# Two plain column tiles instead of four in the first up projection, and a beginning of both up projections ordered by planned times

## The chip, the cores and the metric

The kernel runs on one core of one Trainium2 chip. The metric is the device time of one execution in microseconds; lower is better. The kernel before was timed in three runs, and one more execution was taken with the hardware profiler.

## The reference, cut to what matters

One layer of a hybrid decoder on 512 rows of 1024 columns, all in float32:

```python
def swiglu(x, w_gate, w_up, w_down):
    return (jax.nn.silu(x @ w_gate) * (x @ w_up)) @ w_down

for l in range(DEPTH):                                    # DEPTH = 1
    x = x + 0.5 * swiglu(rmsnorm(x, ffn1_norm[l]), ffn1_wg[l], ffn1_wu[l], ffn1_wd[l])
    x = x + hybrid_mixer(rmsnorm(x, mix_norm[l]), ...)
    x = x + 0.5 * swiglu(rmsnorm(x, ffn2_norm[l]), ffn2_wg[l], ffn2_wu[l], ffn2_wd[l])
return rmsnorm(x, final_norm)
```

The gate and the up matrix of each SwiGLU are 1024 x 2816, so 22 column tiles of 128 each. The change lies in the products with these matrices, in the first SwiGLU and in the second.

## The kernel before, in words

**Precision.** TensorE multiplies float32 in three passes: each operand is split into a rounded part and a remainder (`wh` and `wl` for weights, `yh` and `yl` for the normalised input), and the product of the two remainders is left out. The rounding is a ScalarE copy (`ACTIVATE`), the remainder a VectorE subtraction that waits for it (`wsplit`, L237).

**Plain tiles.** A plain product multiplies one column tile of the gate or of the up matrix (1024 x 128) with all 512 rows: 8 steps of 128 inputs, three matmuls of 512 columns each, 24 in all (`gemm`, L254). The input here is x times the gain; the division by the root mean square is put off: VectorE multiplies the sums with `rstd`. `rstd` comes from `norm_steps` (L289): eight matmuls with a constant matrix (`mean`), a ScalarE square root, a VectorE reciprocal, four transposes on TensorE and a ScalarE copy.

**Units.** The other column tiles are done by a scheme of the Strassen and Winograd kind. A unit takes two column tiles of one matrix (unit `w` those of the gate if `w` is even, those of the up matrix if odd) and cuts inputs, rows and columns in halves. Seven products of half the inputs, half the rows and one tile's columns then stand for eight. Each product has a weight operand (a block of the weights or a sum of blocks: a11, a12, s1 to s4, a22) and a moving operand (`n11`, `b21`, `t2`, `t1`, `r`, `q`, `n22`, each of four parts j). The moving operands are the same for all units, and are built once at the beginning of a projection, out of x, gain and `rstd`, by `moving_operands` (L341): VectorE forms two scaled operands `ca` and `cb` for each j and their differences, ScalarE rounds them, and the remainders are made in three ways: by VectorE, or by a ScalarE copy with the sign turned and an accumulating DMA on GpSimd's queue (`moved`, L359), which lands some microseconds later. All b21, r and q, and t1 and t2 but for the last j, go by DMA.

A unit product of a part j is three matmuls of 256 columns (narrow), or one of 512, which takes the rounded part and the remainder side by side, and one of 256 (wide, L567). Wide products need one more VectorE addition when their bank is read. Here products 2, 5 and 3 are wide in all units (`WIDE`), and all products in the last twelve units of the second projection, whose weight sums are formed ahead in memory (`blocks`). Products 1, 6, 7 and 4 of a unit add up in one bank of PSUM, and ScalarE copies the bank out between them (`results`, L587). `function` (L578) puts a Silu off to the end of the next step in a unit with wide products, and issues it at once in others.

**Order.** Everything in `ffn_up` (L416) is in an order written out by hand: each engine runs its instructions in the order in which the program names them, and semaphores do the waiting. `stream` (L496) lists the products. After product i comes `step(i)` (L665): results of product i - 1, then `prepare(i + LEAD)` with `LEAD = 4`: the rounding and the remainder of the weights of the product four later, and the sums of weights (`add_weights`) of the one after that. Weights rest in three pairs of buffers (`wsp`). `load` fetches a unit's blocks: four or five DMAs from SP's queue and two accumulating DMAs from GpSimd's.

**The beginning before.** With `DIRECT = 4`, the first projection computes column tiles 0 and 1 while the input arrives (four products in `WP` and `pu`), tiles 2 to 5 as eight plain products in `ffn_up`, and tiles 6 to 21 as 16 units. The second computes tiles 0 to 3 as eight plain products and the rest as 18 units. The plain products are what TensorE works on while the norm is finished and the moving operands are built: half a product, one piece of the other work, half a product. The norm's first matmuls stand in the middle of the first plain product, the transposes before the second. The stream before goes unit by unit: 1, 2, 6, 5, 7 of unit 0, then 1 and 2 of unit 1, 4 of unit 0, 6 of unit 1, 3 of unit 0, and so on.

**Halves for the down projection.** Six column tiles of each hidden layer go plain into the down projection and need to be split (`halve`, L739). In the first projection this is done at steps 12, 26, 40, 54, 68 and 82; in the second at 12, 26, 40 and 54, and the last two in the last four steps (L726).

Of the kernel before, what the change touches and what calls it, by code (L numbers as in the profile page):

```python
# [9 lines left out]
F32 = mybir.dt.float32  # L10
F32R = mybir.dt.float32r
# [34 lines left out]
DIRECT = 4  # L46
# [130 lines left out]
def hybrid_kernel(ctx, tc, xt, vec, w1u, w1d, wm, wki, wrg, watt, wrnn, wout, w2u, w2d, gf, out):  # L177
# [163 lines left out]
    def moving_operands(g):  # L341

        moving.update((n, []) for n in ("n11", "b21", "t2", "t1", "r", "q", "n22"))
        held = []

        for k in ("pth", "ptl"):
            t = ptp.tile([P, NQ * S], F32R, tag=k, name=nm("cm"))  # L350
            held.extend(t[:, i * S:(i + 1) * S] for i in range(NQ))

        def rounded(name, src, sign=1.0):
            o = held.pop(0) if len(held) else slot(F32R, "cm")
            moving[name].append(o)
            A.activation(o[:, lo], src, AF.Copy, scale=sign)
            return o, src

        def moved(name, src, soon=False):  # L359
            o, _ = rounded(name, src)  # L360
            if soon:
                V.tensor_sub(o[:, hi], src, f(o[:, lo]))
                return
            A.activation(o[:, hi], src, AF.Copy, scale=-1.0)
            G.dma_start(o[:, hi], src, accum_op=ALU.add)

        def negated(o, src):
            V.scalar_tensor_tensor(o[:, hi], src, -1.0, f(o[:, lo]), op0=ALU.mult, op1=ALU.subtract)

        for j in range(KD // 2):  # L370
            a, b = slot(F32, "ca"), slot(F32, "cb")
            if j % 2 == 0:
                rs, qs = awork("cr"), slot(F32, "cq")
            r, q = (t[:, (lo, hi)[j % 2]] for t in (rs, qs))
            for o, k in ((a, j), (b, j + KD // 2)):
                V.scalar_tensor_tensor(o, x[k], col(g, k), rstd, op0=ALU.mult, op1=ALU.mult)
            n11 = rounded("n11", a[:, lo], -1.0)
            n22 = rounded("n22", b[:, hi], -1.0)
            V.tensor_sub(r, a[:, hi], b[:, hi])
            V.tensor_sub(a[:, hi], a[:, hi], a[:, lo])  # L380
            moved("b21", b[:, lo])
            yield
            negated(*n11)
            V.tensor_sub(a[:, lo], b[:, hi], a[:, hi])
            V.tensor_sub(q, b[:, lo], a[:, lo])
            moved("t1", a[:, hi], j == KD // 2 - 1)
            moved("t2", a[:, lo], j == KD // 2 - 1)
            yield
            negated(*n22)
            moved("r", r)  # L390
            moved("q", q)
            yield

    def ffn_act(pg, pu):
        tg, tu = work("tg"), slot(F32, "h")
        V.tensor_mul(tg, pg, rstd)
        A.activation(tg, tg, AF.Silu)
        V.tensor_mul(tu, pu, rstd)
        V.tensor_mul(tu, tu, tg)
        return tu  # L400
# [6 lines left out]
    def weight_blocks(wu, n0, first):  # L407

        H = KD // 2 * P
        got = {}  # L410
        for w in range(first, KF - n0 - DIRECT):
            u, v = (wu[n0 + DIRECT + w // 2 * 2 + i, w % 2] for i in range(2))
            got[w] = Blocks(u[:, :H], u[:, H:], v[:, :H], v[:, H:])
        return got

    def ffn_up(y, wu, n0, hs, g, waiting=(), given=(), ahead=None, blocks={}, wide=()):  # L416
# [8 lines left out]
        f0 = n0 + DIRECT  # L425
# [16 lines left out]
        def prepare_direct():  # L442
            r = raws[len(split_)]
            h, l = (wsp.tile([P, WMAX], F32R, tag=t, name=nm(t)) for t in ("wh", "wl"))
            split_.append((h, l))
            A.activation(h, r, AF.Copy)
            yield
            V.tensor_sub(l, r, f(h))

        def results_direct(d):  # L450
            n, j = direct[d]
            if j == 0:
                gates.append(work("tg"))
                V.tensor_mul(gates[-1], sums[d], rstd)
                A.activation(gates[-1], gates[-1], AF.Silu)
                yield
            else:
                h = slot(F32, "h")
                V.tensor_mul(h, sums[d], rstd)
                yield  # L460
                V.tensor_mul(h, h, gates.pop())
                hs.append(h)

        def together(*steps):
            steps = list(steps)
            while steps:
                for i in list(steps):
                    try:
                        next(i)
                    except StopIteration:  # L470
                        steps.remove(i)
# [57 lines left out]
        def prepare(i):  # L529
            if i < LEAD:  # L530
                add_weights(i)
            if i + 1 >= LEAD:
                add_weights(i + 1)
# [150 lines left out]

        with tc.manual_schedule(engines=ENGINES):
            for _ in range(len(raws), RAWS + len(raws)):
                fetch()
            together(prepare_direct(), prepare_direct())
            operands, norm = moving_operands(g), norm_steps(acc)
            for d, (n, j) in enumerate(direct):  # L690
                sums.append(psum(("aux", "mm")[n % 2]))
                if d == 1:
                    norm_rest(norm)
                    hs.extend(ffn_act(*p) for p in waiting)
                gemm(sums[d], split_[d], y, range(KD), last=False, upto=KD // 2)
                steps = [results_direct(d - 1)] if d else []
                if d + 2 < len(direct):
                    together(prepare_direct(), *steps)
                    fetch()
                else:  # L700
                    together(*steps)
                    for i in range(2):
                        prepare(2 * (d + 2 - len(direct)) + i)
                if d == 0:
                    for _ in range(3):
                        next(norm)
                if d in (4, 6):
                    load_ = load()
                if d >= 4:
                    next(load_, None)  # L710
                if d > 1:
                    next(operands, None)
                gemm(sums[d], split_[d], y, range(KD), first=False, since=KD // 2)
                if d > 1:
                    next(operands, None)
            for _ in operands:
                pass
            for i in range(len(stream)):
                products(i)
                if not i:  # L720
                    together(results_direct(len(direct) - 1))
                step(i)
                if i + LEAD < len(stream):
                    pass
# [12 lines left out]
            assert not functions  # L737
# [233 lines left out]
    with tc.manual_schedule(engines=ENGINES):  # L971
# [17 lines left out]
        gemm(pu, w, y, range(KD))  # L989
# [4 lines left out]
    ffn_up(y, w1u, 2, hs, V_G1, ((WP[0], WP[1]), (WP[2], pu)), AH[1:], d1.tasks_at, wide=WIDE)  # L994

    BLOCKS2D = down_blocks(w2d)
    BLOCKS2U = weight_blocks(w2u, 0, UNITS)
# [922 lines left out]
    ffn_up(y2, w2u, 0, hs, V_G2, ahead=tasks_at, blocks=BLOCKS2U, wide=WIDE)  # L1920
# [88 lines left out]
```

## Time and profile before

| | us |
|---|---|
| median of three runs | 1066.5 |
| lowest and highest of them | 1065.42, 1066.67 |
| the profiled execution's own time | 1064.61 |
| its span, first to last instruction | 1062.8 |
| TensorE matmul busy | 1052.4 |
| VectorE busy | 881.4 |
| ScalarE busy | 667.0 |
| granted TensorE clock, mean | 0.998 |
| first plain product in `ffn_up`, first and second projection | 27.23, 718.60 |
| first unit product, first and second projection | 72.13, 763.94 |

The views give, for an instruction or a group, the start in microseconds after the span's start, its length, the engine (PE is TensorE, DVE VectorE, ACT ScalarE, POOL GpSimd, SP the DMA queue of SyncE), the operation, "written tile <- read tiles", the shape, and in brackets the time that the engine stood idle before it and who ended that. Matmuls overlap, so the pace is the distance between starts, not the length. Nearly all instructions carry line 171, that of a helper, so tiles tell them apart: `wh` and `wl` are weights, `cm` moving operands, `ca` and `cb` scaled operands, `aux` and `mm` banks of PSUM, `tg` and `tu` a unit's results, `h` hidden tiles, `hh` and `hl` their splits.

### The profile page before, as it was taken

Reading aid. Unit: us, or ns where it says so; the run is one execution under the profiler, and the core shown is the slowest. Engines: PE = TensorE matmul, PEld = TensorE weight load, DVE = VectorE, ACT = ScalarE, POOL = GpSimd, SP = SyncE. Lnnn points to the kernel's source line nnn. Section 1 sums busy time; section 2 is a strip of 40 time slices with the busy share of each in tenths; the row PEclk is TensorE's granted clock in tenths of the full one; section 3 lists DMA queues with packets and bytes.
Section 4 is the critical chain, followed back from the end, with each engine's and each line's share of the span. In section 5 each row is a group of like instructions: output and inputs, shape, how many; then the busy total and the mean of one; then the engine's idle time right before and its main releaser. Section 6 shows DMA issues by size and latency. Waiting matters only on the chain.

```text
span 1062.8 us, 16803 instructions
## 1 busy us (share of the span) xinstructions
PE 1052.4 (99%) x5812; PEld 914.6 (86%) x5812; DVE 881.4 (83%) x1730; ACT 667.0 (63%) x1250; POOL 235.0 (22%) x357
## 2 busy tenths in 40 slices
PE   9999999999999999999999999999999999999997
PEld 7889999989999788888888888888899888888885
DVE  6688888889988879998899867766888888888875
ACT  6565656655576657976886664446656666565663
POOL 0161241102131021212031444442643000000020
PEclk9999999999999999999999999999999999999999
DMA  7398899638794487667594878995997666545573
GB/s 279 73 253 203 212 256 235 163 112 247 173 225 120 127 221 183 171 181 184 135 227 129 215 170 201 268 243 151 250 280 182 200 196 194 183 146 170 188 204 121
DMA packets 93973, 203.71 MB, mean 192 GB/s; under 512 B 11712, under 2 KB 20032, under 8 KB 93248
## 3 DMA queue, kind: packets, MB, share of 16 engines
q1 hardware_dynamic: 60144, 136.24, 39.0%
q0 software_dynamic: 33024, 65.55, 31.9%
q8 instruction: 46, 0.75, 0.3%
q10 hardware_dynamic: 720, 0.84, 0.2%
q14 instruction: 39, 0.32, 0.1%
HBM read 191.58 MB, written 48.23 MB: 226 GB/s over the span
## 4 chain that ended last, share of the span: by engine, by line
PE 90%; DVE 6%; ACT 2%; issue 1%; DMA 1%; ACTq 0%; DVEq 0%
PE mm L171 63%; PE aux L171 27%; DVE wl L171 2%; ACT wh L171 1%; DVE am L171 1%; DVE ca L171 1%; ACT cm L171 1%; DMA wr<-wm 0%; DVE xc L171 0%; DVE h L171 0%; DMA vt<-vec 0%; DVE cb L171 0%; DVE tu L171 0%; DVE tg L171 0%; DVE cm L171 0%
## 5 line engine op out<-in xcount | busy, mean ns | idle before, releaser
L171 DVE TENSOR_TENSOR wl<-wr,wh 128x1024 fp32r<-128x1024 f32 (+2 forms) x241 | 237.8, 990 | 72.3 <-ACT wh L171 70.1
L171 ACT ACTIVATE wh<-wr 128x1024 fp32r<-128x1024 f32 (+3 forms) x243 | 208.4, 864 | 75.6 <-issue 23.6
L171 PE MATMUL mm<-cm,wh 128*128 128x256 f32 (+1 forms) x1280 | 250.4, 300 | 0.0
L171 PEld LDWEIGHTS mm<-cm,wh 128*128 128x128 f32 x1280 | 202.8, 191 | 5.1
L171 PE MATMUL mm<-cm,wl 128*128 128x256 f32 x736 | 184.5, 282 | 0.0
L171 PE MATMUL mm<-yh,wh 128*128 128x512 f32 (+1 forms) x416 | 163.7, 394 | 0.4 <-ACT wh L171 0.2
L171 PE MATMUL mm<-yl,wh 128*128 128x512 f32 (+1 forms) x416 | 162.3, 390 | 0.0
L171 PE MATMUL mm<-yh,wl 128*128 128x512 f32 x408 | 159.3, 390 | 0.0
L171 PEld LDWEIGHTS mm<-cm,wl 128*128 128x128 f32 x736 | 133.7, 191 | 4.1
L171 PE MATMUL aux<-cm,wh 128*128 128x512 f32 (+1 forms) x472 | 123.4, 380 | 0.8 <-ACT cm L171 0.5
L171 PEld LDWEIGHTS mm<-yh,wh 128*128 128x128 f32 (+1 forms) x416 | 78.0, 187 | 17.2 <-ACT i L171 0.6
L171 PEld LDWEIGHTS mm<-yl,wh 128*128 128x128 f32 (+1 forms) x416 | 77.6, 187 | 15.6 <-DVE yl L171 0.5
L171 PEld LDWEIGHTS mm<-yh,wl 128*128 128x128 f32 x408 | 76.6, 188 | 16.3
L171 PEld LDWEIGHTS aux<-cm,wh 128*128 128x128 f32 x472 | 79.8, 190 | 10.8 <-ACT cm L171 0.9
L171 ACT ACTIVATE wh<-s 128x512 fp32r<-128x512 f32 x96 | 59.8, 626 | 41.9 <-DVE s L171 38.4
L171 PEld LDWEIGHTS aux<-cm,wl 128*128 128x128 f32 x440 | 68.7, 189 | 8.6
L171 PE MATMUL aux<-cm,wl 128*128 128x256 f32 x440 | 73.9, 281 | 0.0
L171 DVE TENSOR_TENSOR wl<-s,wh 128x512 fp32r<-128x512 f32 x96 | 64.8, 686 | 5.4 <-ACT wh L171 5.3
L325 POOL DMA_DIRECT2D scr<-w2d x32 | 29.8, 1050 | 174.7 <-DMA scr<-w2d 149.3
L159 POOL DMA_DIRECT2D cm<-h x16 | 13.7, 865 | 205.8 <-ACT cm L171 197.1
L171 PE MATMUL mm<-wh,cm 128*128 128x512 f32 x192 | 59.1, 389 | 0.0
L1010 POOL COPY beat<-beat 128x1 f32<-128x1 f32 x67 | 25.0, 373 | 126.7 <-DVE beat L1009 117.1
(263 smaller groups left out, 2138.3 us busy)
## 6 DMA issues: line engine op xcount, KB each, us to landing
wr<-scr SPq DMA_DIRECT2D x80, 256.0 KB, 3.0
wr<-wm SPq DMA_DIRECT2D x39, 512.0 KB, 4.3
scr<-w2u POOLq DMA_DIRECT2D x72, 256.0 KB, 5.7
wr<-w1u SPq DMA_DIRECT2D x21, 512.0 KB, 5.1
scr<-scr POOLq DMA_DIRECT2D x40, 256.0 KB, 5.3
wr<-w1d SPq DMA_DIRECT2D x18, 512.0 KB, 4.4
wr<-w2u SPq DMA_DIRECT2D x36, 256.0 KB, 3.0
wr<-w2d SPq DMA_DIRECT2D x36, 256.0 KB, 3.0
```

The source lines that it names most:

```text
L159: return self.engine.dma_start(out, src, **kw)
L171: return call(*args, **kw)
L325: plain, adds = nc.gpsimd.dma_start, lambda o, i: nc.gpsimd.dma_start(o, i, accum_op=ALU.add)
L1010: nc.gpsimd.tensor_copy(paces[-1], paces[-1])
```

## The change

`DIRECT` becomes two constants. The first projection now has column tiles 2 and 3 plain (four products) and 18 units; the second keeps four plain tiles and 18 units.

In both, what runs beside the plain products and the first unit products becomes a list of events, each with a planned time. They are sorted by it and issued in that order; the times make an order and nothing waits for them. Time 0 is the first plain matmul, `T0` the planned end of the plain products, and before unit product i all events up to `T0` + 1.42 i are issued.

The first two units' products come in turn (1 of unit 0, 1 of unit 1, 2 of unit 0, 2 of unit 1, then 6, 5 and 7 likewise), and these two units have no wide products. Their first weight blocks are loaded into two slots rather than a raw buffer, earlier than before. The remainders of `b21` and `t2` are all made by VectorE; all of `t1`, `r` and `q` go by DMA. The moving operands are built in smaller pieces (`scaled`, `first`, `second`, `third`). The plain results are handled per tile, gate and up together. The norm's first matmuls move: in the first projection to before the last three steps of the product `pu`, in the second from behind four to behind five steps of the first plain product. All six halves are split at steps 12 to 82 in both projections.

```diff
-DIRECT = 4
+DIRECT1, DIRECT2 = 2, 4
...
+    class Operands:
...
+        def scaled(self, j):
+            for got, name, k in ((self.a, "ca", j), (self.b, "cb", j + KD // 2)):
+                got.append(slot(F32, name))
+                V.scalar_tensor_tensor(got[j], x[k], col(self.g, k), rstd, op0=ALU.mult, op1=ALU.mult)
+            self.rounded("n11", j, self.a[j][:, lo], -1.0)
+            self.rounded("b21", j, self.b[j][:, lo])
...
+        def second(self, j):
+            a, b = self.a[j], self.b[j]
             V.tensor_sub(a[:, lo], b[:, hi], a[:, hi])
...
+            self.rounded("t2", j, a[:, lo])
...
-            o.wide = range(1, 8) if o.blocks else wide
+            o.wide = range(1, 8) if o.blocks else wide if w > 1 else ()
...
-            if blocks and w + 2 >= min(blocks):
+            if w < 2 or blocks and w + 2 >= min(blocks):
...
-        for w in range(count):
-            stream += [(1, w), (2, w)] + [(4, w - 1)] * (w > 0) + [(6, w)]
-            stream += [(3, w - 1)] * (w > 0) + [(5, w), (7, w)]
+        for p in (1, 2, 6, 5, 7):
+            stream += [(p, 0), (p, 1)]
+        stream += [(1, 2), (4, 0), (2, 2), (4, 1), (6, 2), (3, 0), (3, 1), (5, 2), (7, 2)]
+        for w in range(3, count):
+            stream += [(1, w), (2, w), (4, w - 1), (6, w), (3, w - 1), (5, w), (7, w)]
...
+        D, K = 24 * 0.2267, 3 * 0.2267
+        T0, R = len(direct) * D, norm_at[-1] + 1.3
...
+        t = max(R, T0 - 21.5)
+        for n, banks in enumerate(waiting):
+            at(R + n, result_direct, "w%d" % n, *banks)
+            at(R + 0.5 + n, result_direct, "w%d" % n)
+            at(R + 4.6 + n / 2, result_direct, "w%d" % n)
+            t = R + 2.4
...
+        for j in range(KD // 2):
+            at(t, ops.scaled, j)
+            at(t + 1.35, ops.first, j)
+            at(t + 2.1, ops.negated, "n11", j)
+            at(t + 2.5, ops.moved, "t1", j)
+            t += 2.5
+            at(T0 - 2.5, ops.remainder, "b21", j)
+            at(T0 - 2.2, ops.second, j)
+            at(T0 - 2.0 + 1.3 * j, ops.moved, "r", j)
+            at(T0 - 0.6, ops.remainder, "t2", j)
+            at(T0 + 4.3 + 1.4 * (j // 2), ops.third, j)
+            at(T0 + 5.7 + 1.4 * (j // 2), ops.moved, "q", j)
+            at(T0 + 13 + 1.4 * (j // 2), ops.negated, "n22", j)
+        for i in range(LEAD):
+            at(T0 - 3.5 + i // 2, prepare, i)
+        at(T0 - 0.2, add_weights, LEAD)
+        for d in range(0, len(direct), 2):
+            t = T0 + 4.4 + 2.2 * (d + 4 - len(direct)) if d + 4 >= len(direct) else (d + 2) * D + 1
+            at(t, lambda d=d: result_direct(d, *sums[d:d + 2]))
+            at(t + 1.4, result_direct, d)
+            at(t + 2.8, result_direct, d)
...
             for i in range(len(stream)):
+                begin(T0 + i * 1.42)
                 products(i)
-                if not i:
-                    together(results_direct(len(direct) - 1))
                 step(i)
-                if i + LEAD < len(stream):
-                    pass
-                elif not ahead or i + LEAD - len(stream) < PLAIN - f0:
-                    halve(hs, f0 + i + LEAD - len(stream))
...
-                if i % 14 == 12 and i // 14 < f0:
+                if i % 14 == 12 and i // 14 < PLAIN:
                     halve(hs, i // 14)
...
-        gemm(pu, w, y, range(KD))
+        norm1 = norm_steps(acc)
+        gemm(pu, w, y, range(KD), last=False, upto=5)
+        next(norm1)
+        gemm(pu, w, y, range(KD), first=False, since=5)
```

More of the change, by code (lines that the diff above doesn't have):

```diff
@@ L392, in moving_operands, with third @@
[L392 to L400, printed above, removed]
+            self.rounded("t2", j, a[:, lo])
+        def third(self, j):
+            if j % 2 == 0:
+                self.qs.append(slot(F32, "cq"))
+            V.tensor_sub(self.q(j), self.b[j][:, lo], self.a[j][:, lo])
     class W:
@@ L405, in hybrid_kernel, with weight_blocks, ffn_up @@
     WIDE = (2, 5, 3)
-    def weight_blocks(wu, n0, first):
+    def weight_blocks(wu, f0, first):
         H = KD // 2 * P
         got = {}
-        for w in range(first, KF - n0 - DIRECT):
-            u, v = (wu[n0 + DIRECT + w // 2 * 2 + i, w % 2] for i in range(2))
+        for w in range(first, KF - f0):
+            u, v = (wu[f0 + w // 2 * 2 + i, w % 2] for i in range(2))
             got[w] = Blocks(u[:, :H], u[:, H:], v[:, :H], v[:, H:])
         return got
-    def ffn_up(y, wu, n0, hs, g, waiting=(), given=(), ahead=None, blocks={}, wide=()):
+    def ffn_up(y, wu, n0, tiles, hs, g, norm, norm_at, waiting=(), given=(), ahead=None, blocks={}, wide=()):
         H = KD // 2 * P
-        f0 = n0 + DIRECT
+        f0 = n0 + tiles
         count = KF - f0
@@ L440, in fetch, with round_direct, rest_direct, results_direct @@
                 raws.append(r)
[L442 to L446, printed above, removed]
-            yield
[L448 to L471, printed above, removed]
+        def round_direct(d):
+            split_.append(tuple(wsp.tile([P, WMAX], F32R, tag=t, name=nm(t)) for t in ("wh", "wl")))
+            A.activation(split_[d][0], raws[d], AF.Copy)
+        def rest_direct(d):
+            V.tensor_sub(split_[d][1], raws[d], f(split_[d][0]))
+        def results_direct(g_, u_):
+            tg, h = work("tg"), slot(F32, "h")
+            V.tensor_mul(tg, g_, rstd)
+            V.tensor_mul(h, u_, rstd)
+            yield
+            A.activation(tg, tg, AF.Silu)
+            yield
+            V.tensor_mul(h, h, tg)
+            hs.append(h)
         def load():
@@ L683, in step, with product_direct, load_first @@
                 A.activation(t, t, AF.Silu)
+        D, K = 24 * 0.2267, 3 * 0.2267
+        T0, R = len(direct) * D, norm_at[-1] + 1.3
+        ops, events, loads, direct_results = Operands(g), [], {}, {}
+        at = lambda t, fn, *args: events.append((t, len(events), fn, args))
+        def product_direct(d, k):
+            if k == 0:
+                sums.append(psum(("aux", "mm")[direct[d][0] % 2]))
+            gemm(sums[d], split_[d], y, range(KD), since=k, upto=k + 1)
+        def load_first(w):
+            if w not in loads:
+                loads[w] = load()
+            next(loads[w], None)
@@ L687, in ffn_up @@
                 fetch()
[L688 to L716, printed above, removed]
-                pass
+            for d in range(2):
+                round_direct(d)
+                rest_direct(d)
+                fetch()
+            events.sort()
+            load_ = iter(())
             for i in range(len(stream)):
+                begin(T0 + i * 1.42)
                 products(i)
-                if not i:
-                    together(results_direct(len(direct) - 1))
                 step(i)
-                if i + LEAD < len(stream):
-                    pass
-                elif not ahead or i + LEAD - len(stream) < PLAIN - f0:
-                    halve(hs, f0 + i + LEAD - len(stream))
                 if ahead:
                     ahead(i - len(stream))
-                if i % 14 == 12 and i // 14 < f0:
+                if i % 14 == 12 and i // 14 < PLAIN:
                     halve(hs, i // 14)
@@ L736, in ffn_up @@
             step(len(stream))
-            assert not functions
+            assert not functions and not events
     def halve(hs, n):
@@ L1918, in hybrid_kernel @@
         then(lastD + m + 1, scaled, m)
-    ffn_up(y2, w2u, 0, hs, V_G2, ahead=tasks_at, blocks=BLOCKS2U, wide=WIDE)
+    ffn_up(y2, w2u, 0, DIRECT2, hs, V_G2, norm_steps(acc), (2.73, 3.2, 3.4, 4.78, 5.3), ahead=tasks_at, blocks=BLOCKS2U, wide=WIDE)
     with tc.manual_schedule(engines=ENGINES):
```

97 lines of the change are left out of this document (57 added, 40 removed).

## The prediction

> **What bounds the kernel now.** First the page.
>
> ```profile
> span 1062.8 us, 16803 instructions
> PE 1052.4 (99%) x5812; PEld 914.6 (86%) x5812; DVE 881.4 (83%) x1730; ACT 667.0 (63%) x1250; POOL 235.0 (22%) x357
> PE 90%; DVE 6%; ACT 2%; issue 1%; DMA 1%; ACTq 0%; DVEq 0%
> ```
>
> TensorE is busy 99% of the span and carries 90% of the chain that ended last. So there are two ways to gain: fewer TensorE passes, or fewer of the short gaps. VectorE at 83% is the engine that can become the bound. The chain in order of time gives the pace of the products:
>
> ```profile
> 78.80 2.87 PE mm L171 x24
> 81.67 1.40 PE aux L171 x8
> ...
> 88.75 2.88 PE mm L171 x24
> ...
> 753.22 10.89 PE mm L171 x48
> ```
>
> Two plain products (48 matmuls) take 10.88, one 5.44. Two narrow unit products take 2.87, one 1.435; a wide one takes 1.40. A unit of seven products recurs after 88.75 - 78.80 = 9.95. TensorE's timeline then shows the gaps at the beginnings and at the end of the second up projection:
>
> ```profile
> 73.56 0.86 PE L171 MATMUL aux<-cm,wh 128*128 128x512 f32 x3
> 74.89 0.47 PE L171 MATMUL aux<-cm,wh 128*128 128x512 f32 x1 [0.48 <-ACT cm L171]
> ...
> 75.70 0.50 PE L171 MATMUL mm<-cm,wh 128*128 128x256 f32 x2
> ...
> 721.09 0.39 PE L171 MATMUL aux<-yh,wl 128*128 128x512 f32 x1
> 721.69 1.13 PE L171 MATMUL aux<-mean,acc 128*128 128x128 f32 x8 [0.21 <-DVE acc L171]
> ...
> 765.37 0.86 PE L171 MATMUL aux<-cm,wh 128*128 128x512 f32 x3
> 766.58 0.47 PE L171 MATMUL aux<-cm,wh 128*128 128x512 f32 x1 [0.35 <-ACT wh L171]
> ...
> 767.36 0.40 PE L171 MATMUL mm<-cm,wh 128*128 128x256 f32 x2
> ...
> 944.92 0.40 PE L171 MATMUL aux<-wl,hh 128*128 128x512 f32 x1
> 945.80 0.50 PE L171 MATMUL aux<-wh,hh 128*128 128x512 f32 x1 [0.48 <-DVE e L171]
> ```
>
> The first wide product of the first up projection takes 75.70 - 73.56 = 2.14 where 1.40 is the pace: 0.74 lost. In the second it takes 1.99: 0.59 lost. The mean's matmuls start 0.60 after the matmul before them, where one pass is 10.88 / 48 = 0.23: 0.37 lost. At 945.80 it is 0.88 for 0.23: 0.65 lost. Together 2.35.
>
> **The change, part by part.**
>
> *Two units for two plain tiles.* Four plain products (4 x 5.44 = 21.76) go and two units (2 x 9.95 = 19.90) come: -1.86.
>
> *First two units narrow.* Products 2, 5 and 3 of two units in each projection, 12 in all, cost 1.435 for 1.40: +0.42. [...]
>
> *The two operand waits.* The last b21 remainder is formed by an accumulating DMA on POOL's queue:
>
> ```profile
> 69.55 0.86 POOL L159 DMA_DIRECT2D cm<-cb  x1 [1.55 <-ACT cm L171]
> ...
> 761.30 0.86 POOL L159 DMA_DIRECT2D cm<-cb  x1 [3.02 <-PE mm L171]
> cm<-cb POOLq DMA_DIRECT2D x4, 128.0 KB, 5.3
> cm<-cq POOLq DMA_DIRECT2D x4, 128.0 KB, 6.9
> ```
>
> 69.55 + 5.3 = 74.85 and 761.30 + 5.3 = 766.60: the two gaps end where those DMAs land, not on ScalarE. The change gives b21 and t2 to VectorE, so both gaps go: -1.33. POOL issues 12 operand DMAs instead of 18; it is 22% busy, so nothing comes of that. What is late next is VectorE, below.
>
> *The mean's wait.* In the second up projection its matmuls go behind five steps of eight instead of four, 0.68 later, which covers the 0.37: -0.37. In the first they move ahead, into the last product before it:
>
> ```profile
> 29.95 1.05 PE L171 MATMUL aux<-mean,acc 128*128 128x128 f32 x8
> 31.34 0.18 DVE L171 RECIPROCAL rs<-sd 128x4 f32<-128x4 f32 x1 [1.81 <-ACT sd L171]
> ```
>
> From the mean's end (31.00) to the reciprocal's (31.52) are 0.5, and the three steps left behind it (3 x 0.68) cover that. If acc is late there, it costs up to the same 0.37; I take 0.
>
> *The tail of the second up projection.* Two halves of plain tiles are split there, and go to steps 68 and 82:
>
> ```profile
> 937.85 0.69 DVE L171 TENSOR_TENSOR hl<-h,hh 128x512 fp32r<-128x512 f32 x1 [1.01 <-ACT hh L171]
> ...
> 941.47 0.69 DVE L171 TENSOR_TENSOR hl<-h,hh 128x512 fp32r<-128x512 f32 x1
> ```
>
> They are two VectorE subtractions and one wait of 1.01 in the eight microseconds before the gap at 945.80, more than its 0.65: -0.65. Where they go, the windows show VectorE with room:
>
> ```profile
> 92.00:112.00 20.00, 20.00 (x146) 18.94 (x145) 17.76 (x36) 11.85 (x26) 5.45 (x7) 1.00 0.73 188
> 786.00:830.00 44.00, 44.00 (x310) 41.17 (x309) 38.05 (x84) 24.96 (x48) 16.66 (x31) 1.00 0.86 219
> ```
>
> The third figure after the stretch is VectorE's: 38.05 of 44. The same rows say that in the steady units of the first projection it has 2.2 of 20 to spare, about 1.1 a unit.
>
> *Loads.* SP queues the first two units' blocks up to 20 us earlier, each first block as two transfers; the DMA share of the steady rows is 0.73 to 0.86, so 0, at most 0.5.
>
> So far: -1.86 + 0.42 - 1.33 - 0.37 - 0.65 = -3.79.
>
> *The new beginning.* Half the cover is gone: four plain products (21.8) instead of eight. I put the instructions of VectorE and ScalarE in the order of the diff, each with its pace from these rows (start to start):
>
> ```profile
> 33.58 0.60 PE L171 MATMUL aux<-ident,rs 128*128 128x128 f32 x4
> 33.93 0.48 PE L171 MATMUL aux<-yh,wh 128*128 128x512 f32 x1
> 34.22 0.60 ACT L171 ACTIVATE rstd<-aux 128x512 f32<-128x512 f32 x1 [2.91 <-PE aux L171]
> 34.84 0.69 DVE L171 TENSOR_TENSOR tg<-mm,rstd 128x512 f32<-128x512 f32 x1 [3.33 <-ACT rstd L171]
> 35.45 0.68 DVE L171 TENSOR_TENSOR h<-mm,rstd 128x512 f32<-128x512 f32 x1
> ...
> 48.75 1.23 DVE L171 TENSOR_TENSOR wl<-wr,wh 128x1024 fp32r<-128x1024 f32 x1 [1.05 <-ACT wh L171]
> 49.89 0.42 DVE L171 SCALAR_TENSOR_TENSOR cm<-cb,cm 128x256 fp32r<-128x256 f32 x1
> 50.23 0.74 DVE L171 SCALAR_TENSOR_TENSOR ca<-x,vt,rstd 128x512 f32<-128x512 f32 x1
> 50.89 0.75 DVE L171 SCALAR_TENSOR_TENSOR cb<-x,vt,rstd 128x512 f32<-128x512 f32 x1
> ...
> 64.20 1.14 ACT L171 ACTIVATE wh<-wr 128x512 fp32r<-128x512 f32 x2
> 65.25 0.71 ACT L171 ACTIVATE cm<-cr 128x256 fp32r<-128x256 f32 x2
> ```
>
> VectorE: 0.61 for 512 columns, 1.14 for 1024, 0.34 for 256 (0.45 where it needs the one before), 0.66 for a scaled operand. ScalarE: 0.53 for 512, 0.31 for 256. Zero is the first plain matmul; rstd is there at 34.82 - 33.93 = 0.9.
>
> VectorE from 0.9: the two waiting tiles 6 x 0.61, two plain remainders 2 x 1.14, eight scaled operands 8 x 0.66, and per operand pair 0.45 + 0.34 + 0.34: 15.8 in all, to 16.7. It waits for ScalarE's rounding of the first unit weights until 17.9. Then four unit remainders, the b21, `second` and t2 steps (12 x 0.34) and two weight sums, 7.7: to 25.6. TensorE began unit products at 21.8. ScalarE stood from 19.3 until `second` gave it its first t2 source at 22.0; its list up to the weights of product 5 (t2 roundings, r copies, two bank copies, three weight roundings) is 6.3 long, to 28.5, and VectorE waits 1.9 for pieces of it. From 28.6 VectorE has three unit remainders, two bank subtractions, four q subtractions and the plain tile's two products with rstd, 5.1: the last q at 33.7. ScalarE copies q first and then product 6's bank, done at 35.1. Product 7 of unit 0 adds into that bank and is due at 21.8 + 8 x 1.44 = 33.3. **TensorE waits 1.8.**
>
> Behind that, the narrow units issue their Silu at once (the branch of `function` for units without `wide`), where wide ones put it off one step. ScalarE then stands 1 to 2.3 for VectorE, which is some 4 us behind, and the next weight roundings wait behind it. Carried on, this gives 0.2 and 0.4 before product 4 of units 0 and 1, 0.8 before 6 of unit 2, 0.4 before 3 of unit 0 and 0.9 before 4 of unit 2: 2.7. In the second projection no tiles wait and the norm's matmuls (1.2) lie after zero, so VectorE is some 3 us better off: the wait at product 7 goes, and of the later ones 0.5, 0.4 and 0.9 stay, 1.8. The sum of new waits is 1.8 + 2.7 + 1.8 = 6.3.
>
> The bounds: nothing, if VectorE and ScalarE run a tenth quicker than the rows; 8, if each beginning is 0.7 later (q landing after 6.9 instead of being there when needed). No gain beyond nothing is possible, as the gaps removed are counted already. I take 6.3.
>
> **Sum.** -3.79 + 6.3 = +2.5. The profiled execution takes 1064.61 (span 1062.8 and 1.8 around it), which is 1.9 below the median of the three runs, 1066.5. So the profile after should show about 1067.1, and the median is 1066.5 + 2.5 = 1069.0.
>
> **Rivals.** *A, the queues keep ahead.* Weights are prepared four products, 5.7 us, ahead; VectorE's pure work, without its waits, always ends over 2 us before it is due; and the kernel before ran its beginnings on the same tight queues without waiting for VectorE. It decides at product 6's bank copy: if that ends by 33.3, 1.8 sooner than I place it, most later waits shrink too. Then -3.8: 1062.7. This is the case on the other side.
>
> *B, half of it.* ScalarE's stand before t2 is shorter, or only the first wait appears: new waits of 1.7 to 5.9 leave the time within 2.1 of before, 1066.5 at the middle. For it: the later waits are a few tenths each, no more than the error of such a layout.
>
> *C, the planned times do not hold.* They are an order, not a wait: an engine that is early does not stop, one that is late holds all behind it. If VectorE is late by 0.7 more in each projection, TensorE waits 1.4 more: 1070.4. For it: ScalarE and VectorE hand over some hundredths slower in the trace than in a layout.
>
> **Chances.** 0.2% is 2.1 us, about what a measurement of this kernel can tell from no change. Forecast 0.29 and C 0.15, both slower, 0.44; B 0.28, within 0.2%; A 0.28, faster. The range that leaves out 2 in 10 runs from just above A's time to just above that of the upper bound (-3.79 + 8 = +4.2, 1070.7): 1063.0 to 1071.0. The forecast's own case is 1068.6 to 1070.
>
> **What the changed profile would show.** Right: 18 units at 9.95 in the first projection; no wait for a `cm` DMA at its first wide products; no gap for acc near 722 nor for `e` near 945; a gap of 1 to 3 us some 11 us after the first unit product, before an `mm` product, ended by ScalarE; ScalarE idle before the t2 roundings. Wrong, if TensorE runs through both beginnings without idle time (then A), or if the lost time lies at the plain products or in loads of the first units.

## The result, and the profile after

The changed kernel takes 1073.7 us (median of 6 runs, 1072.36 to 1074.65), the one before 1066.24 in the same comparison (6 runs): 1.007 times as long, 95% interval 1.0058 to 1.0082. It is slower by 7.5 us. The prediction said slower, by 2.5, with 1071.0 as its upper end; the sign was right and the size was not. The profiled execution took 1074.0, with a span of 1072.2. That is 9.4 us of span more than before, 1.9 more than the medians differ by, because the execution of before that was profiled, 1064.61, was 1.6 quicker than the median and this one 0.3 slower.

First the page of the changed kernel.

```profile
span 1072.2 us, 17013 instructions
PE 1055.3 (98%) x5908; PEld 920.6 (86%) x5908; DVE 887.3 (83%) x1753; ACT 668.8 (62%) x1255; POOL 227.8 (21%) x349
PE 89%; DVE 5%; DMA 2%; issue 2%; ACT 1%; POOL 0%; ACTq 0%; POOLq 0%; DVEq 0%
```

The shares differ from before by one point at most: the DMA's share of the chain has gone from 1% to 2%, "issue" likewise, and TensorE, VectorE and ScalarE have lost a point each. So the question is where on TensorE's timeline the 9.4 us of span lie. The first rows that read a moving operand (`cm`) or a split hidden tile (`hh`) mark the stages. In TensorE's timeline of before:

```profile
72.13 0.40 PE L171 MATMUL mm<-cm,wh 128*128 128x256 f32 x2
232.29 0.40 PE L171 MATMUL aux<-hh,wh 128*128 128x512 f32 x1
763.94 0.40 PE L171 MATMUL mm<-cm,wh 128*128 128x256 f32 x2
942.98 0.47 PE L171 MATMUL aux<-wh,hh 128*128 128x512 f32 x1
```

and of after:

```profile
51.15 0.40 PE L171 MATMUL mm<-cm,wh 128*128 128x256 f32 x2
235.27 0.40 PE L171 MATMUL aux<-hh,wh 128*128 128x512 f32 x1
766.52 0.40 PE L171 MATMUL mm<-cm,wh 128*128 128x256 f32 x2
953.02 0.47 PE L171 MATMUL aux<-wh,hh 128*128 128x512 f32 x1
```

| stage, us | before | after | difference |
|---|---|---|---|
| span's start to first unit product | 72.13 | 51.15 | -20.98 |
| units of the first up projection (16, then 18) | 160.16 | 184.12 | +23.96 |
| to the first unit product of the second | 531.65 | 531.25 | -0.40 |
| units of the second (18) | 179.04 | 186.50 | +7.46 |
| rest of the span | 119.82 | 119.18 | -0.64 |

The first projection as a whole is 3.0 longer (-20.98 + 23.96). Two units at 9.95 are 19.90 of the 23.96; with 0.21 for six narrow products, and with the 0.74 of before gone, 4.6 of new waits are left. The second projection has 7.46 - 0.21 + 0.59 = 7.8 of new waits. These are not alike. In the first, TensorE's timeline shows many short waits, ended by ScalarE and VectorE:

```profile
64.35 0.51 PE L171 MATMUL mm<-cm,wh 128*128 128x256 f32 x2 [1.53 <-ACT tg L171]
...
74.61 0.39 PE L171 MATMUL mm<-cm,wl 128*128 128x256 f32 x1 [0.59 <-DVE wl L171]
...
76.49 0.39 PE L171 MATMUL aux<-cm,wl 128*128 128x256 f32 x1 [0.18 <-DVE wl L171]
...
85.79 0.50 PE L171 MATMUL mm<-cm,wh 128*128 128x256 f32 x2 [0.74 <-ACT tg L171]
```

In the second there is one place, product 4 of unit 0, and the releaser is a DMA:

```profile
782.36 0.28 PE L171 MATMUL mm<-cm,wh 128*128 128x256 f32 x1
786.09 0.39 PE L171 MATMUL mm<-cm,wh 128*128 128x256 f32 x1 [3.45 <-DMA cm<-cq]
...
787.47 0.58 PE L171 MATMUL mm<-cm,wh 128*128 128x256 f32 x1 [0.77 <-DMA cm<-cq]
...
788.88 0.58 PE L171 MATMUL mm<-cm,wh 128*128 128x256 f32 x1 [0.40 <-DMA cm<-cq]
...
790.11 1.91 PE L171 MATMUL aux<-cm,wh 128*128 128x512 f32 x4
```

The first matmul of the product, on q's rounded half, starts on time at 782.36; the second needs the remainder that an accumulating DMA forms in the other half, and waits. The three waits are for the first three of q's four parts. The product takes 790.11 - 782.36 = 7.75 instead of 1.435. And the four wide matmuls at 790.11 take 1.91 where before they took 1.09. That is the clock, as the windows show (after the stretch: PE, PEld, DVE, ACT, POOL busy, then the granted clock, the DMA share and GB/s):

```profile
782.00:786.00 4.00, 0.64 (x6) 0.43 (x4) 3.56 (x9) 3.10 (x9) 3.11 (x4) 1.00 1.14 278
...
787.00:788.00 1.00, 0.53 (x2) 0.53 (x3) 1.00 (x5) 0.30 (x1) 0.68 (x2) 0.50 1.20 302
...
790.00:792.00 2.00, 2.00 (x7) 1.61 (x7) 0.72 (x2) 1.65 (x4) 0.00 (x0) 0.50 1.09 264
...
794.00:800.00 6.00, 6.00 (x49) 5.82 (x48) 3.24 (x8) 3.21 (x6) 0.00 (x0) 1.00 0.48 113
```

TensorE does nothing for 3.5 us, and soon after it starts again its clock is at half, until it is back at full speed by 794. Why q is late shows on the timelines of ScalarE, which copies q, and of GpSimd, which issues the DMAs:

```profile
772.95 1.32 ACT L171 ACTIVATE cm<-cq 128x256 fp32r<-128x256 f32 x4
...
772.06 1.84 POOL L159 DMA_DIRECT2D s<-w2u  x2
775.05 0.30 POOL L1042 COPY beat<-beat 128x1 f32<-128x1 f32 x1 [1.15 <-DVE beat L1041]
775.30 0.82 POOL L325 DMA_DIRECT2D scr<-w2u  x1
775.84 2.97 POOL L159 DMA_DIRECT2D cm<-cq  x3
779.32 0.86 POOL L159 DMA_DIRECT2D cm<-cq  x1 [0.52 <-ACT wh L171]
```

`scr` and `beat` belong to `sums_until`, which runs after every second step of the second up projection: it forms weight sums of the last twelve units by DMA in a scratch memory, and paces them with a mark, a VectorE memset followed by a GpSimd copy that waits for it. q's DMAs stand in that queue behind a mark and its transfer: the copies of q's first two parts are done by 774.27, and the first DMA goes out at 775.84. The part is due at about 782.5, behind the first matmul of the product, and lands at 786.0; TensorE goes on at 786.09. The last of the four goes out at 779.32 and holds nothing up. So q is issued late, and it also takes long to land. The DMA view of the 8 us from 774:

```profile
q0 software_dynamic: 683, 1.23, 83.9%
...
cm<-cq POOLq DMA_DIRECT2D x4, 128.0 KB, 10.6
```

In the first projection, the 8 us from 59 (q's first DMA goes out at 60.91), the same lines read

```profile
q0 software_dynamic: 989, 1.16, 95.1%
...
cm<-cq POOLq DMA_DIRECT2D x4, 128.0 KB, 4.1
```

The third figure of the queue's line is the time that its packets took, as a share of 16 DMA engines. q lands after 10.6 us instead of 4.1, although by this figure GpSimd's queue is the less full of the two, so this share does not tell how long q takes. The single transfers tell more. In the trace of the changed kernel GpSimd's transfers land here in the order in which they were issued (start of each plus its own time to landing): the second `s` at 782.6, `scr` at 784.6, and the first three parts of q at 786.0, 787.4 and 788.8. So q lands behind what was issued before it, and these parts follow each other by 1.4 us, against 0.7 to 0.8 in the first projection.

The other gaps of before are gone as foretold. The mean's matmuls of the second projection follow the matmul before them at its pace (725.03 behind 724.80), and the split plain tiles stand in the last steps no more:

```profile
724.80 0.39 PE L171 MATMUL aux<-yh,wl 128*128 128x512 f32 x1
725.03 1.05 PE L171 MATMUL aux<-mean,acc 128*128 128x128 f32 x8
...
951.75 0.63 PE L171 MATMUL aux<-cm,wl 128*128 128x256 f32 x4
952.23 1.03 PE L171 MATMUL mm<-ident,x 128*128 128x128 f32 x8
953.02 0.47 PE L171 MATMUL aux<-wh,hh 128*128 128x512 f32 x1
```

### The profile page after: what moved, and what is told of

It reads as the page before. It is cut to its first block, busy times and chain, and to the rows that moved or that the text cites. A ratio compares the mean times of both kernels' runs of the same rounds, so it can differ in the third digit from the quotient of the medians.

```text
span 1072.2 us, 17013 instructions
## 1 busy us (share of the span) xinstructions
PE 1055.3 (98%) x5908; PEld 920.6 (86%) x5908; DVE 887.3 (83%) x1753; ACT 668.8 (62%) x1255; POOL 227.8 (21%) x349
## 4 chain that ended last, share of the span: by engine, by line
PE 89%; DVE 5%; DMA 2%; issue 2%; ACT 1%; POOL 0%; ACTq 0%; POOLq 0%; DVEq 0%
PE mm L171 63%; PE aux L171 26%; DVE wl L171 1%; DMA cm<-cq 1%; DVE am L171 1%; DVE h L171 1%; DMA wr<-wm 0%; DVE xc L171 0%; DMA wr<-w1u 0%; DMA cm<-cr 0%; DVE ca L171 0%; DVE tg L171 0%; ACT wh L171 0%; DVE cb L171 0%; DVE tu L171 0%
## 5 line engine op out<-in xcount | busy, mean ns | idle before, releaser
L171 DVE TENSOR_TENSOR wl<-wr,wh 128x1024 fp32r<-128x1024 f32 (+2 forms) x233 | 230.2, 992 | 73.8 <-ACT wh L171 71.7
L171 PE MATMUL mm<-cm,wh 128*128 128x256 f32 (+1 forms) x1344 | 264.2, 300 | 7.0 <-DMA cm<-cq 4.6
L171 ACT ACTIVATE wh<-wr 128x1024 fp32r<-128x1024 f32 (+3 forms) x235 | 202.1, 865 | 76.4 <-issue 23.8
L171 PEld LDWEIGHTS mm<-cm,wh 128*128 128x128 f32 x1344 | 213.9, 192 | 13.5 <-DMA cm<-cq 5.3
L171 PE MATMUL mm<-cm,wl 128*128 128x256 f32 x768 | 194.1, 283 | 0.6 <-DVE wl L171 0.6
L171 PEld LDWEIGHTS mm<-cm,wl 128*128 128x128 f32 x768 | 140.4, 192 | 4.9 <-DVE wl L171 0.8
L171 PE MATMUL aux<-cm,wh 128*128 128x512 f32 (+1 forms) x544 | 134.7, 363 | 0.0
L171 PEld LDWEIGHTS aux<-cm,wh 128*128 128x128 f32 x544 | 91.2, 191 | 8.8
L171 PE MATMUL aux<-cm,wl 128*128 128x256 f32 x464 | 84.1, 282 | 0.2 <-DVE wl L171 0.2
L159 POOL DMA_DIRECT2D s<-w1u x36 | 32.7, 1084 | 130.2 <-DMA s<-w1u 54.3
```

Source lines behind the costliest of these rows:

```text
L159: return self.engine.dma_start(out, src, **kw)
L171: return call(*args, **kw)
```

## The experiments

The theories. Theory 1: the size was missed because q's accumulating DMAs land late in the second projection, behind the sums in GpSimd's queue, and the clock falls in the wait. Theory 2: VectorE and ScalarE are behind in both beginnings, and the DMA is only the last of several late things. Medians of before in these comparisons are 1065.6 to 1065.7, so ratios are given where they decide.

**e1, q by VectorE in the second projection.**

```
-            at(T0 + 5.7 + 1.4 * (j // 2), ops.moved, "q", j)
+            at(T0 + 5.7 + 1.4 * (j // 2), ops.moved, "q", j, bool(blocks))
...
+            if soon:
+                self.remainder(name, j)
+                return
```

> The changed kernel, except that in the second up projection q's four remainders are subtracted on VectorE (4 x 0.34 us) instead of being formed by ScalarE negations and accumulating DMAs on POOL's queue. Theory 1 (q's DMAs land late there, and TensorE's clock falls in the wait): the 3.45 + 0.77 + 0.40 us of waits before product 4 of unit 0 go, the granted clock stays at 1.00, and of the 7.8 us lost in this stage 5 to 7 come back: 1067 to 1069 (1073.7 for the changed kernel). What stays are waits of a few tenths on VectorE. Theory 2 (VectorE and ScalarE are behind, and the DMA is only the last of several that are late): VectorE gets 1.4 us more, the wait moves to it, and the time stays within 1.5 of 1073.7.

Measured: 1067.58 (10 runs), ratio to before 1.002, interval 1.0011 to 1.003. The 18 units take 946.28 - 766.23 = 180.05 instead of 186.50, the mean granted clock is 0.998, as in the kernel before (0.996 in the changed kernel), and one wait is left in TensorE's timeline of the second projection:

```profile
797.62 0.51 PE L171 MATMUL mm<-cm,wh 128*128 128x256 f32 x2 [0.74 <-ACT tg L171]
```

Theory 1 holds: 6.1 us of the medians' 7.5 come back (5.3 by the ratios), although VectorE does more.

**e2, the sums held back for 14 steps.**

```
-                if blocks and i % 2 == 0:
+                if blocks and i % 2 == 0 and i >= 14:
                     sums_until(...)
```

> The changed kernel, except that the sums of weight blocks by DMA (their pace marks on VectorE and POOL, and their transfers from scratch) are held back over the first 14 steps of the second up projection and made up for at step 14. q's remainders still come by DMA. Theory 1a (contention: the sums' transfers fill the DMA engines and POOL's ring): q's DMAs land in 4 to 7 us instead of 10.6, the wait falls from 4.6 to under 2, and the time is 3 to 6 lower, 1068 to 1071. Theory 1b (POOL issues q late, behind the marks, and the landing is long for other reasons, such as the units' own accumulations): issue comes 1 to 1.5 us earlier, landing stays over 9, time about 1.5 lower, 1072. Theory 2: no change, 1073 to 1074.

**e11, held back for three steps only.**

```
-                if blocks and i % 2 == 0:
+                if blocks and i % 2 == 0 and i not in (2, 4, 6):
```

> The changed kernel with the sums of weight blocks held back at steps 2, 4 and 6 of the second up projection only, so that q's DMAs go out on POOL ahead of the pace marks and transfers of these steps, which follow from step 8 on. Theory 1a (the sums' transfers lengthen the landing): it falls from 10.6 towards the 7.0 of e2_sums_held, at least under 8.5, and with the earlier issue the wait of 4.6 falls under 2: 1067.5 to 1070. Theory 1b (only the issue counts): q is issued 1 to 1.5 earlier, lands after 9.5 to 11 all the same, the wait stays 2.5 to 4: 1070.5 to 1072.5.

Measured: e2 1071.2 (4 runs), ratio 1.0052 (1.0036 to 1.0069); e11 1069.37 (5 runs), ratio 1.0034 (1.002 to 1.0048). Both times lie where theory 1a puts them. In e2, q's DMAs go out from 774.16 to 777.70 instead of 775.84 to 779.32, and the DMA view of its 8 us from 772 has

```profile
q0 software_dynamic: 505, 0.73, 55.2%
...
cm<-cq POOLq DMA_DIRECT2D x4, 128.0 KB, 7.0
```

With the sums held back q lands in 7.0 and TensorE waits 0.49. e2 does not gain all of it: the sums made up for at step 14 go out just ahead of an accumulating load (`s`) of a later unit, which lands after 10.0, and TensorE stands there (the first line is the longest piece of the chain that ended last, in this stretch):

```profile
799.52 9.97 DMA s<-w2u
...
811.72 0.50 PE L171 MATMUL mm<-cm,wh 128*128 128x256 f32 x2 [2.83 <-ACT tu L171]
```

In e11 q lands in 7.7, the two waits for it are 0.51 and 0.80, no other is left in this projection, and the 18 units take 948.69 - 768.09 = 180.6, 5.9 less than 186.50. The matching 8 us, from 773.7, read

```profile
q0 software_dynamic: 887, 1.16, 86.3%
...
cm<-cq POOLq DMA_DIRECT2D x4, 128.0 KB, 7.7
```

Counted from the first unit product, q's first DMA goes out 7.4 behind it in e11 (775.51 - 768.09) and 9.3 in the changed kernel (775.84 - 766.52): 1.9 earlier to issue, 2.9 shorter to land. Both parts count. The queue is as full in e11 as in the changed kernel (86.3% and 83.9%), so that share does not account for the landing. What e11 took away is the `scr` in front of q: without it q's first part lands 1.3 behind `s` (782.7 and 781.4), in the changed kernel 3.4 behind it (786.0 and 782.6). From one part to the next it is 1.2 to 1.4 in e11 too. In both, loads of SP's queue are in flight beside q: from 766 to 800 that queue's packets took 34.6% of the DMA engines' time in e11 and 28.8% in the changed kernel. No run takes these away, and why the parts land twice as far apart as in the first projection stays open.

**e3, the wait filled with other matmuls.** (They add into columns of a bank that nothing reads.)

```
+            if blocks and (p, w) == (4, 0):
+                for _ in range(38):
+                    T.matmul(both[:, hi], h[:, :P], moving["n11"][0][:, lo], start=False, stop=False, ...)
```

> The changed kernel with 38 matmuls of 128x256 more (4.6 us at 0.12 each), ahead of product 4 of unit 0 in the second up projection, which add into columns of its bank that nothing reads. They need none of q. Theory 1: TensorE stays busy while q's DMAs land, so the granted clock stays near 1.00 where it was 0.59 (786 to 790) and 0.82 (790 to 800), and the products behind the wait run at pace: 1 to 2.5 lower, 1071.2 to 1072.7, although there is more work. If the slow products behind the wait have another cause than the clock (operands, weights): no gain, 1073.5 to 1075.

Measured: 1070.96 (4 runs), 2.7 below the changed kernel with 38 matmuls more; the 18 units take 951.29 - 766.91 = 184.38, 2.1 less. TensorE's timeline:

```profile
782.75 4.96 PE L171 MATMUL mm<-cm,wh 128*128 128x256 f32 x40
...
788.88 0.38 PE L171 MATMUL mm<-cm,wh 128*128 128x256 f32 x1 [0.57 <-DMA cm<-cq]
...
789.92 1.08 PE L171 MATMUL aux<-cm,wh 128*128 128x512 f32 x4
```

q is as late as before, with a median landing of 10.2, but the wide matmuls behind it take 1.08, not 1.91, and the mean granted clock is 0.998, not 0.996. So of the 7.8 lost there, the wait itself is some 5.5 and the clock 2 to 2.7.

**e4, four plain tiles in the first projection again.**

```
-DIRECT1, DIRECT2 = 2, 4
+DIRECT1, DIRECT2 = 4, 4
```

> The changed kernel with four plain column tiles in the first up projection again (16 units), its beginning in the new order and its first two units narrow. If the waits there (1.53 at product 7 of unit 0, 0.59, 0.18, 0.74 later, with the slow matmul starts after them 4.8 in all) come from the shorter cover (21.8 us of plain products instead of 43.5), they go: -4.8 + 1.86 for the two plain tiles, about -3, 1070.7. If they come from the order and the narrow units themselves, they stay and the time is +1 to +2: 1074.7 to 1075.7. The second up projection is the same in both, with its wait for q of about 8.

Measured: 1071.72 (4 runs), 2.0 below the changed kernel. The waits at 64.35, 74.61 and most of 76.49 have no counterpart; one of 0.73, ended by `tg`, stays (at 104.90), and 0.15 for `wl`. The first unit product comes 21.85 later (73.00 for 51.15), but the first `hh` row comes 0.81 earlier (234.46 for 235.27). So the shorter cover costs more than the two tiles save, and a part, 161.46 - 160.16 = 1.3 against before, belongs to the order and the narrow units.

**e5, the narrow units' Silu behind the next weight roundings of its step** (on top of e1).

```
             else:
-                A.activation(t, t, AF.Silu)
+                soon.append(t)
...
-            for t in ready:
+            for t in ready + soon:
```

> The changed kernel with q's remainders by VectorE in the second up projection (1067.6 so far), and the Silu of the two narrow units put behind the next weight roundings of its step on ScalarE, instead of ahead of them. Theory, as the prediction has it (ScalarE stands at the Silu for VectorE, and the next weight roundings wait behind it): the waits of 0.73 and 0.74 before a unit product that ScalarE's tg ends (at 85.45 and 797.62), and part of 0.58 and 0.18, go: 1 to 2.5 lower, 1065 to 1066.6. Rival (VectorE is what is late, and ScalarE would stand at the next instruction just the same): within 0.5 of 1067.6.

Measured: 1064.86 (11 runs), 2.7 below e1, ratio 0.9995 (0.9986 to 1.0004). In the second projection no wait is left, and the 18 units take 943.88 - 765.23 = 178.65, which is before's 179.04 - 0.59 + 0.21 to a hundredth. In the first, 1.52 at product 7, 0.45 and 0.19 stay. The theory holds, a little beyond its range.

**e6, q behind the copy of product 6's bank in the first projection; e9, q by VectorE there too; e10, the same at the old planned time; e12, only its last two by VectorE.**

```
-            at(T0 + 5.7 + 1.4 * (j // 2), ops.moved, "q", j, bool(blocks))
+            at(T0 + (5.7 if blocks else 7.2) + 1.4 * (j // 2), ops.moved, "q", j, bool(blocks))           # e6
+            at(T0 + (5.7 if blocks else 7.2) + 1.4 * (j // 2), ops.moved, "q", j, True)                   # e9
+            at(T0 + 5.7 + 1.4 * (j // 2), ops.moved, "q", j, True)                                        # e10
+            at(T0 + (5.7 if blocks else 7.2) + 1.4 * (j // 2), ops.moved, "q", j, bool(blocks) or j > 1)  # e12
```

> The kernel of e5_silu_behind, with q's copies in the first up projection planned 1.5 us later, which puts them behind the copy of product 6's bank on ScalarE; their DMAs go out as much later. Theory (product 7 of unit 0 waits because that copy stands behind q's): the wait of 1.51 at product 7 goes, and q still lands before it is due, 4.1 us after its issue: 1.3 to 1.9 below e5, 1063.5 to 1065. Rival (q is then late, as in the second projection): the wait moves from product 7 to product 4 of unit 0, and the time is as for e5 or higher.

> The kernel of e6_q_behind_copy with q's remainders by VectorE in the first up projection too, at the same planned times (behind the copy of product 6's bank). Theory (in e6 the wait of 1.56 at product 4 of unit 0 is q's accumulating DMAs alone, issued too late to land in time; VectorE has the 1.4 us that the four subtractions take): the wait goes, 1.0 to 1.8 below e6 (1064.1), so 1062.3 to 1063.1, and with two plain tiles for four it is at or below e8 (1063.1). Rival (VectorE is full there): a wait for wl or for ScalarE's copies of 1 to 2 us takes its place, 1063.5 to 1065.

> The kernel of e5_silu_behind with q's remainders by VectorE in the first up projection too, and q at the changed kernel's planned times, ahead of the copy of product 6's bank. ScalarE has four copies of 0.31 less ahead of that copy, but still stands for VectorE's q. Theory (product 7 waits because the copy is queued behind q, which VectorE gives late): the wait of 1.52 at product 7 falls by 0.6 at most, or stays, since VectorE also has the remainders ahead; the time is 1064 to 1065.5. Rival (ScalarE's eight copies are the length of it): the wait falls under 0.5 and the time to 1063 to 1063.7.

> The kernel of e6_q_behind_copy with the last two of q's four remainders of the first up projection by VectorE (2 x 0.34 us); the first two stay with accumulating DMAs. In e6 the wait of 1.56 stood inside product 4 of unit 0 and ended on the third operand, whose DMA was issued at 64.8 and landed 4.8 later; the first two were there. Theory (these two DMAs alone are late, and VectorE can take 0.7 us more but not the 1.4 of e9, where a wait of 1.19 for tg took its place): the wait goes and none over 0.6 replaces it, 0.8 to 1.6 below e6's 1064.1: 1062.5 to 1063.3, level with e8 or below it. Rival (VectorE is full there already): waits for tg or wl of about 1 take its place, 1063.7 to 1064.7.

Measured (11 runs each): e6 1064.11, ratio 0.9987 (0.9978 to 0.9996); e9 1064.36, 0.9988 (0.9979 to 0.9997); e10 1065.33, 0.9997 (0.9988 to 1.0006); e12 1063.74, 0.9983 (0.9974 to 0.9992). Where TensorE then waits in the first projection, in e6:

```profile
69.68 0.39 PE L171 MATMUL mm<-cm,wh 128*128 128x256 f32 x1 [1.56 <-DMA cm<-cq]
```

and in e9:

```profile
66.97 0.47 PE L171 MATMUL mm<-cm,wh 128*128 128x256 f32 x2 [1.19 <-DVE tg L171]
```

In e6 the wait at product 7 is gone, and q's DMA, sent later, is late in its place: the rival. Only the smaller waits, 0.45 and 0.19, went with it. With q on VectorE (e9) VectorE is late instead, and in e12 a wait of 0.70 for `tg` with 0.45 and 0.18 for `wl` stay: a wait over 0.6 takes the place of the first, and the time lies where the rival puts it. In e10 the wait at product 7 is 1.60: fewer ScalarE copies of q do not shorten it. But VectorE, with the remainders in front, starts its last two subtractions of q 0.7 later there (63.00 - 51.25 = 11.75 behind the first unit product for 62.24 - 51.15 = 11.09), so e10 does not tell the copies from VectorE's lateness, which the prediction named. None of the four orders finds 1.5 us of room in that beginning.

**e7, three parts of the change in the old order.**

```
-            moved("b21", b[:, lo])
+            moved("b21", b[:, lo], j == KD // 2 - 1)
...
+                cut = KD // 2 + (d == 0 and not waiting)
...
-                elif not ahead or i + LEAD - len(stream) < PLAIN - f0:
-                    halve(hs, f0 + i + LEAD - len(stream))
...
-                if i % 14 == 12 and i // 14 < f0:
+                if i % 14 == 12 and i // 14 < PLAIN:
```

> The kernel before with three parts of the change alone: the last b21 remainder by VectorE instead of an accumulating DMA, the mean's matmuls of the second up projection behind five steps of eight, and the halves of the last two plain tiles at steps 68 and 82. Four plain tiles, the old order and the wide units stay. By the prediction's terms (0.74 + 0.59, 0.37, 0.65) it is 2.35 faster than before: 1063.4 with 1065.7 for before. If these parts only move a wait to the next late operand, it is within 0.8 of before.

Measured: 1064.07 (11 runs), ratio 0.9991 (0.9982 to 0.9999): 1.0 to 1.5 faster, not 2.35. The tail gives 0.68 (119.14 for 119.82) and the second projection's units 0.63 (178.41 for 179.04), as expected. In the first, the 0.74 for b21's DMA is replaced by the next late thing, a bank copy on ScalarE before the next product:

```profile
76.21 0.50 PE L171 MATMUL mm<-cm,wh 128*128 128x256 f32 x2 [0.91 <-ACT tg L171]
```

**e8, e6 with four plain tiles in the first projection.** The edit is that of e4.

> The kernel of e6_q_behind_copy with four plain column tiles in the first up projection again. If the waits of the first projection are gone in e6, the two plain tiles cost 1.86 and buy nothing: e6 + 1.3 to e6 + 1.9. If the short cover still costs there, as in the changed kernel, where four tiles came out 2.0 lower, it is below e6 by up to 2.

Measured: 1063.11 (11 runs), ratio 0.998 (0.9971 to 0.9989). Neither up projection has a wait of TensorE left that the timeline marks, and from 783 to 803, where VectorE is busy 19.54 of 20 us, TensorE is busy all 20.00. It beats both kernels: 2.1 below before by the ratio, 2.5 by the medians, and 10.6 below the changed one. Against e6 it is 1.0 lower, so what the two plain tiles save on TensorE, 1.86, is lost to the shorter cover, and 1.0 more; from e12 it can't be told apart.

## Why the prediction was right and wrong

*Two units for two plain tiles, -1.86; narrow units, +0.42.* The 18 units that run free of waits in e5 take 178.65, as the two paces foretell, and between e4 and the changed kernel the two plain tiles are 21.85 long (21.76). Right. The stage before the units is 20.98 shorter, not 21.76: 0.25 is the mean's (below), 0.53 lies ahead of 8.5 us, while the input arrives, and its cause stays open.

*The two operand waits, -1.33.* No wait for b21 is left in either projection. What is late next in the first was counted in the new waits; e7 shows that without the new beginning it would have been 0.91.

*The mean's wait, -0.37, and the tail, -0.65.* The stages shrink by 0.40 and 0.64. Right. In the first projection acc is late before the mean (25.85 behind 25.47, for 0.23), which with a slower start behind it (0.91 to the next matmul, 0.81 in the kernel before) costs 0.25; I had taken 0 of at most 0.37.

*The first projection's new waits, 4.5.* The sum is 4.6. Place by place, a start's delay against the pace of the row before it: 1.69 at product 7 of unit 0 (1.8 predicted), 0 and 0.27 at product 4 of units 0 and 1 (0.2 and 0.4), 0.74 at 6 of unit 2 (0.8), 0.34 at 3 of unit 0 (0.4), 0.90 at 4 of unit 2 (0.9); 0.16 at product 1 of unit 2 and a tenth behind each stop (from the start at 64.35 to the next row 0.34, where 0.24 is the pace) make up the rest. Laying out the two engines' queues with the durations of the rows was good to a few tenths, and e4 and e5 confirm its two reasons, the short cover and the Silu. One step of it is not accounted for: VectorE is at 25.6 + 1.9 = 27.5 and goes on from 28.6, and without that 1.1 the wait at product 7 would have come out at 0.7. Rivals A and B, which had the queues keep ahead, are out.

*The second projection's new waits, 1.8.* **This is the step that failed**: 7.8 came. For VectorE and ScalarE alone it was good: the wait at product 7 did not appear, and with q off the DMAs (e1) 1.4 us of waits stay, 0.91 of them at product 4 of unit 2 as placed (797.62 against 796.71). But I had put q there "when needed", and only in the upper bound at 6.9. That figure is the median of the first projection's four parts in the kernel before; its DMA view of the second, 720 to 780, has

```profile
cm<-cq POOLq DMA_DIRECT2D x4, 128.0 KB, 7.9
```

Of GpSimd the prediction says "POOL issues 12 operand DMAs instead of 18; it is 22% busy, so nothing comes of that". Its busy share was no measure. What counted was the order of its queue, where q had moved behind the marks and transfers of `sums_until`. In the kernel before, the q DMAs of the second projection were all issued by 766.6, ahead of the first `scr` transfer there:

```profile
765.42 1.15 POOL L159 DMA_DIRECT2D cm<-cq  x1
766.93 0.57 POOL L1010 COPY beat<-beat 128x1 f32<-128x1 f32 x1 [0.36 <-DVE beat L1009]
767.44 0.83 POOL L325 DMA_DIRECT2D scr<-w2u  x1
```

The layout had VectorE's last q 33.7 - 21.8 = 11.9 behind the first unit product in the first projection and some 3 earlier in the second, so near 9 (the trace has 775.23 - 766.52 = 8.7). Product 4 of unit 0 was due 11 x 1.44 = 15.8 behind it. Between lie ScalarE's copies and the issue, so some 5 us were left to land, by an estimate from these rows, less than either median. That the sign came out right is not luck: with q off the DMAs the kernel is still 1.9 slower than before (e1), near the 2.5 of the forecast.

*The clock* was no term of the sum. After the wait of 3.45 us it stood at 0.50 from 787 to 793, which cost 2 to 2.7 us more (e3). In e4 a wait of 3.21, also for q, was followed by 0.50 from 787 to 793 as well. Around the wait of 1.53 in the first projection the windows from 60 to 70 have 1.00 throughout, and e2's profiled execution, with its wait of 2.83, has a mean of 0.998 over the span, as the kernel before. What sets the clock back after one wait and not after another was not shown.

*Rival C* had the right sign, and not the mechanism: VectorE was not later by 0.7 in each projection.

## What to carry to other kernels

When a step is moved, lay out every queue that it passes, the one that issues its DMAs as well, and take the landing time from the stretch where the transfer will run, not from a median: the same 128 KB took 4.1 us in one place and 10.6 in another. An engine that is 21% busy can still be the one that holds an operand up: here q's first DMA went out at 775.84, 1.57 us after the copies of q's first two parts were done, behind a mark that waited 1.15 for VectorE and behind the transfer of that mark, and it landed behind that transfer too (786.0 and 784.6). And a wait on TensorE can cost more than its length: in the changed kernel the clock of 0.50 after the wait of 3.45 us cost 2 to 2.7 us on top.

## What the runs showed of the hardware

An accumulating DMA of 128 KB from GpSimd's queue lands in 4.1 us where that queue's packets take 95% of the DMA engines' time, in 7.0 at 55% (e2), in 7.7 at 86% (e11) and in 10.6 at 84%, medians of q's four, each over 8 us: in these four the time does not follow the share. In the changed kernel's second projection the queue's transfers land in the order of issue, from the second `s` at 782.6 to q's third part at 788.8, and q's first three parts some 1.4 us apart. After TensorE has stood for 3.21 us (e4) or 3.45 us the granted clock falls to 0.50 about 0.6 to 1.1 us after it starts again, and in the changed kernel stays there for 6 to 7 us; in e2's profiled execution, with a wait of 2.83 us, the mean over the span is 0.998, as in the kernel before.
